# Last slab of down takes its first five weights for both token blocks in turn; x1's transposes at half the rate

## The chip, the cores and the metric

The kernel runs on one core of one Trainium2 chip. Its time is device microseconds of one execution; lower is better. A core has TensorE (PE) for matrix products, with its weight loads listed apart (PEld), VectorE (DVE), ScalarE (ACT), GpSimd (POOL) and SyncE (SP). Here SP issues most of the DMAs, and POOL some. Each engine works through its own instructions strictly in order: an instruction that waits holds up all that stand behind it.

## The reference, cut to what matters

One residual block, float32, 2048 tokens of 1024 channels. The part that the change touches is the second half: the down projection, the norm behind it and the residual.

```python
x = x + rmsnorm(merged @ w_o[l], norm_mix_post[l])        # called x1 below
h = rmsnorm(x, norm_mlp_pre[l])
f = jnp.square(jax.nn.relu(h @ w_up[l])) @ w_down[l]      # 2048x4096 @ 4096x1024
x = x + rmsnorm(f, norm_mlp_post[l])
```

Ahead of it stand one combined input projection of the normed x, a pooling branch, a convolution branch, and their gated sum `merged`.

## The kernel before, in words

**Tiling.** Tokens come in two blocks b of 1024, each of two halves t of 512 (T); rows g of a half are 128 tokens. Matrix products follow a fast 2x2 scheme of seven products i = 1 to 7, whose operands are a block or a sum of blocks of the weight and of the tokens. For precision each operand is a high part plus a low part, both of a type that TensorE takes at full pace, and three of the four partial products are computed (high by high, high by the tokens' low, the weight's low by high).

**down.** Its 4096 rows are four slabs s, the last of which is `LAST`. A slab has 7 products for each token block. The list `jobs` (1898) is the order of all of them; its first entry is done earlier, so that 55 jobs remain, the last 14 of them in the last slab. A job is two halves h of 24 matmuls, 48 in all (`token_product`, the matmul is L1708). It takes two weight tiles o = 0, 1 and two token cells j. A weight tile is a raw tile `wr` that SP loads, ACT's cast of it to `wh` (L209 before the last slab, L1647 in it), and a low part `wl`: in the earlier slabs DVE subtracts it (L123), and in the last slab SP loads it from `lows` in DRAM, where `last_weights` (1570) has put it, with weight sums in `wsum`. A token cell is a load from `fd` into a `tr` buffer, ACT's cast of it (L1688) and DVE's subtraction into the same `tr` buffer (L123). Cells are prepared two jobs ahead in the last slab, one ahead elsewhere. Buffers rotate: 5 `wr`, 3 `wh`, 3 `wl`, 9 `tr`, 28 `big`, 5 `fo`. All `load` calls go to SP (L129), all `aside` calls to POOL (L133).

**The last slab.** In the earlier slabs each product's sum is added to an accumulator in `acc` by DVE (L120). In the last slab `last_product` (1745) keeps sums open in PSUM, a chain for each h: products 1, 6, 7, 4 go on in one chain, 5 and 3 in another, 2 has its own, and after each product DVE adds the chain as it stands into one quadrant of the output. A quadrant (m, t) is a half m of the channels and a half t of the tokens. `ENDS` names the product after which each quadrant is complete. The jobs of the last slab run all seven products of b = 0, then all seven of b = 1, so each weight is fetched twice. The main loop (1940) asks for both weight tiles of a job right ahead of it.

**Background.** Generators in `lanes` run beside the jobs: after each half job `bg()` steps every lane, so two steps to a job. A step lets a lane advance its generator `rate` times; `yield n` makes it sit out n steps. Two matter here. `turned` (1770) brings x1 from its transposed layout `x1d` into rows `x1t` in 16 rounds: two loads on POOL into a `tr` buffer, a wait of `yield 2`, one transpose on DVE (L1784) into a second `tr` buffer, four stores on POOL. `Finish` (1798) ends one quarter [b, t] of the output: `gain` sums the squares and applies the channel gains for each complete quadrant, `fetch` loads rows of `x1t` into `big` buffers on SP, `root` forms the norm, `cell` (L1831) scales and adds the residual on DVE, `put` stores. `steps` does that for three of the quarters; for [1, 1], `last_steps` prepares and `at_end` finishes inside the last product. Which of the instructions that are ready goes first is settled when the program is built, by priority: weights and cells are put forward (`AHEAD`), background work behind; the engines then run what that gives, in order.

The lines that the change touches:

```python
    DOWN_LAST = (1, 6, 7, 4, 2, 5, 3)                                  # 1566
                        yield 2                                        # 1783
            for g in range(2):                                         # 1846
                self.fetch(g)
    jobs += [(LAST, i, b) for b in range(NB) for i in DOWN_LAST]       # 1901
```

Of the kernel before, what the change touches and what calls it, by code (L numbers as in the profile page):

```python
# [67 lines left out]
def block_kernel(  # L68
# [1496 lines left out]
    DOWN = (5, 6, 1, 3, 7, 4, 2)  # L1565
    DOWN_LAST = (1, 6, 7, 4, 2, 5, 3)
    ENDS = {(0, 0): 2, (1, 0): 4, (1, 1): 5, (0, 1): 3}
    wsum, lows = {}, {}
# [176 lines left out]
    def last_product(i, h, b, w, cells):  # L1745

        if i in (1, 2, 5):
            if i == 5 and b:
                chains[i, h] = [root_psum() if h else psum("down")[:, :T] for _ in (0, 1)]
            else:  # L1750
                tiles[i, h] = psum("down")
                chains[i, h] = banks(tiles[i, h])
        of = {1: 1, 6: 1, 7: 1, 4: 1, 2: 2, 5: 5, 3: 5}[i]
        ps, whole = chains[of, h], tiles.get((of, h))
        final = (i, b) == (DOWN_LAST[-1], 1)
# [14 lines left out]
    def turned():  # L1770
        for b in range(NB):
            for t in (0, 1):
                to = x1t[b, t].rearrange("(n tb i) (q k j) -> n q i tb k j", n=2, i=32, q=4, j=32)
                for c in (0, 2):
                    for n in (0, 1):
                        x, y = mk(*TR), mk(*TR)
                        s = slice(n * (T // 2), (n + 1) * (T // 2))
                        for k in (0, 1):
# [3 lines left out]
                            )  # L1782
                        yield 2
                        nc.vector.transpose(  # L1784
# [13 lines left out]
    class Finish:  # L1798
# [38 lines left out]
        def put(self, g):  # L1837
            (load if self.b else aside)(out[self.b, self.t, g], self.x[g])

        def steps(self, lag):  # L1840
            for k in ((0, 0), (0, 1), (1, 0), (1, 1)) if self.t == 0 else ((1, 0), (1, 1), (0, 0), (0, 1)):
                while k not in self.ready:
                    yield 1
                self.gain(*k)
                yield
            for g in range(2):
                self.fetch(g)
            r = self.root(0, G)
            yield lag
            for g in range(G):  # L1850
                if g + 2 < G:
                    self.fetch(g + 2)
                self.cell(g, r[:, g : g + 1], self.parts(g))
                self.put(g)
                yield

        def last_steps(self):
            for g in range(G):
                self.fetch(g)
            for k in ((1, 0), (1, 1)):  # L1860
                while k not in self.ready:
                    yield 1
                self.gain(*k)
                yield

        def at_end(self, h, c, ps):
# [17 lines left out]
            def after(gg):  # L1884
                with tc.high_priority(offset=URGENT):
                    arrive(gg)
                    if gg:
                        r = self.root(2 * h, 2 * h + 2)
                        for g in (0, 1):
                            leave(2 * h + g, r[:, g : g + 1])  # L1890

# [48 lines left out]
    for n, (s, i, b) in enumerate(jobs):  # L1940
        if s < LAST and i == DOWN[0] and b == 0:
            part = weights_down(s)
        if s == LAST and i == DOWN_LAST[0]:
            part = weights_down(s)
            if b == 0:
# [96 lines left out]
```

## Time and profile before

| what | value |
|---|---|
| time, median of 3 runs | 2176.47 us (2173.34 to 2177.3) |
| the profiled execution's own time | 2174.86 us |
| its span, first to last instruction | 2173.1 us |
| its mean granted TensorE clock | 0.995 |
| PE busy | 2135.3 us, 98%, 9424 matmuls |
| DVE busy | 1716.1 us, 79% |
| ACT busy | 1034.3 us, 48% |
| POOL busy | 74.8 us, 3% |
| DMA | 578.54 MB, mean 266 GB/s |

The span is that of one execution on record, and the trace's times count from its start. Busy shares are averages over stages that differ. The stage of the down products is the last quarter of the span; its rows are read by windows and waits below. In a row of waits the arrow points from what stood still to what released it, `<-`; in an instruction's row, the brackets hold its idle time and what ended it. Queue names with a small q at the end (SPq) mean the issuing of DMAs.

### The profile page before, as it was taken

To read this page: it belongs to the slowest core of one execution; us is meant where nothing else is said; L and a number is where in the kernel's file an instruction comes from. 1 tells how busy PE (TensorE), PEld (TensorE's weight loads), DVE (VectorE), ACT (ScalarE), POOL (GpSimd) and SP (SyncE) were. 2 spreads that over 40 slices of the span, in tenths; PEclk is the share of its full clock that TensorE was granted. 3 is DMA by queue.
4 is the path that set the end of the run, shared out by engine and by line. 5 is a ranking of instruction groups with operands and counts; after the bars stand their busy time and mean duration, and the time that the engine had idled before them with its cause. 6 is when DMAs were issued, how large, how long until landed. Compare 5 with 4: busy or idle time off the path is not lost.

```text
span 2173.1 us, 25018 instructions
## 1 busy us (share of the span) xinstructions
PE 2135.3 (98%) x9424; PEld 1759.1 (81%) x9424; DVE 1716.1 (79%) x1664; ACT 1034.3 (48%) x1119; POOL 74.8 (3%) x131
## 2 busy tenths in 40 slices
PE   9999999999999999999999999999999999999996
PEld 7778888888888888888888888888887788888875
DVE  8999788999789999997777857876655775687557
ACT  6444453334534655445635766665443332223442
POOL 0000000000000000000000000000122300000000
PEclk9999999999999999999999999999999999999998
DMA  4789998688897787336686768986987775445896
GB/s 177 267 301 330 342 353 311 228 286 305 320 342 271 262 303 268 136 116 233 249 335 227 267 249 307 360 284 240 345 277 280 257 257 173 163 145 187 298 365 235
DMA packets 167498, 578.54 MB, mean 266 GB/s; under 512 B 20304, under 2 KB 24528, under 8 KB 167376
## 3 DMA queue, kind: packets, MB, share of 16 engines
q1 hardware_dynamic: 145616, 501.42, 64.4%
q10 hardware_dynamic: 12672, 46.14, 5.5%
q0 software_dynamic: 9088, 29.37, 3.9%
q8 instruction: 74, 1.21, 0.2%
q14 instruction: 48, 0.39, 0.1%
HBM read 381.20 MB, written 195.65 MB: 265 GB/s over the span
## 4 chain that ended last, share of the span: by engine, by line
PE 73%; DVE 9%; DMA 9%; issue 5%; ACT 2%; POOL 1%; SPq 0%; DVEq 0%; ACTq 0%; POOLq 0%
PE up L252 28%; PE down L1708 18%; PE wo L252 7%; PE glu L252 5%; PE B L252 4%; PE ga L252 3%; PE gb L252 3%; DVE y L910 3%; PE pool L252 2%; DMA tr<-x1d 2%; PE A L252 2%; DMA wl<-lows 1%; DMA tr<-fd 1%; POOL x1t L133 1%; DVE wl L123 1%
## 5 line engine op out<-in xcount | busy, mean ns | idle before, releaser
L252 PE MATMUL up<-big,wh 128*128 128x512 f32 x1792 | 480.9, 390 | 1.2 <-DVE big L123 0.8
L252 PEld LDWEIGHTS up<-big,wh 128*128 128x128 f32 x1792 | 335.8, 188 | 71.9 <-DVE big L123 1.1
L209 ACT CAST wh<-wr 128x1024 fp32r<-128x1024 f32 x167 | 175.5, 1052 | 314.9 <-PE up L252 68.5
L1708 PE MATMUL down<-wh,tr 128*128 128x512 f32 x784 | 307.0, 392 | 3.2 <-DVE tr L123 3.2
L910 DVE SCALAR_TENSOR_TENSOR y<-v,cst,y 128x1024 f32<-128x1024 f32 x240 | 307.0, 1279 | 2.4
L1708 PE MATMUL down<-wh,fo 128*128 128x512 f32 x776 | 298.6, 390 | 0.5 <-ACT wh L209 0.5
L252 PE MATMUL up<-big,wl 128*128 128x512 f32 x896 | 275.9, 389 | 0.0
L1708 PE MATMUL down<-wl,fo 128*128 128x512 f32 x760 | 235.1, 391 | 3.0 <-DVE wl L123 3.0
L209 ACT CAST wh<-ws 128x1024 fp32r<-128x1024 f32 x124 | 130.5, 1053 | 220.1 <-PE up L252 74.7
L252 PEld LDWEIGHTS up<-big,wl 128*128 128x128 f32 x896 | 168.2, 188 | 35.1
L1688 ACT CAST fo<-tr 128x1024 fp32r<-128x1024 f32 x86 | 90.4, 1051 | 219.2 <-DMA tr<-fd 90.8
L123 DVE TENSOR_TENSOR wl<-ws,wh 128x1024 fp32r<-128x1024 f32 x116 | 141.4, 1219 | 46.8 <-ACT wh L209 46.3
L1708 PEld LDWEIGHTS down<-wh,tr 128*128 128x128 f32 x784 | 148.0, 189 | 35.2 <-DVE tr L123 4.3
L1708 PEld LDWEIGHTS down<-wh,fo 128*128 128x128 f32 x776 | 145.9, 188 | 31.4 <-ACT wh L209 0.9
L1708 PEld LDWEIGHTS down<-wl,fo 128*128 128x128 f32 x760 | 142.7, 188 | 34.6 <-DVE wl L123 5.3
L123 DVE TENSOR_TENSOR wl<-wr,wh 128x1024 fp32r<-128x1024 f32 x111 | 135.1, 1218 | 26.0 <-ACT wh L209 22.9
L120 DVE TENSOR_TENSOR big<-big,down 128x1024 f32<-128x1024 f32 (+1 forms) x84 | 99.8, 1189 | 70.4 <-PE down L1708 70.3
L123 DVE TENSOR_TENSOR tr<-tr,fo 128x1024 fp32r<-128x1024 f32 x86 | 104.7, 1219 | 46.2 <-ACT fo L1688 46.0
L252 PE MATMUL glu<-big,wh 128*128 128x512 f32 x432 | 117.5, 393 | 3.0 <-ACT tr L408 2.5
L252 PE MATMUL wo<-big,wh 128*128 128x512 f32 x448 | 120.2, 390 | 0.0
L252 PE MATMUL gb<-big,wh 128*128 128x512 f32 x448 | 120.1, 390 | 0.0
L252 PE MATMUL ga<-big,wh 128*128 128x512 f32 x448 | 119.8, 389 | 0.0
(208 smaller groups left out, 3383.0 us busy)
## 6 DMA issues: line engine op xcount, KB each, us to landing
tr<-fd SPq DMA_DIRECT2D x110, 512.0 KB, 4.5
wr<-w_down SPq DMA_DIRECT2D x68, 512.0 KB, 6.3
wl<-kept SPq DMA_DIRECT2D x67, 512.0 KB, 5.2
kept<-wl SPq DMA_DIRECT2D x66, 512.0 KB, 5.7
wr<-w_up SPq DMA_DIRECT2D x64, 512.0 KB, 4.5
wr<-w_in SPq DMA_DIRECT2D x56, 512.0 KB, 6.0
fd<-tr ACTq DMA_DIRECT2D x54, 512.0 KB, 3.5
fd<-tr SPq DMA_DIRECT2D x48, 512.0 KB, 3.3
```

What stands on the lines that cost most here:

```text
L120: return nc.vector.tensor_tensor(o, a, b, op=ALU.add)
L123: return nc.vector.tensor_tensor(o, a, b, op=ALU.subtract)
L133: return nc.gpsimd.dma_start(o, src)
L209: nc.scalar.copy(hi[:, :n], src[:, :n])
L252: i = nc.tensor.matmul(ps, w[wp][:, (at + k) * P : (at + k + 1) * P], rhs[k][xp], start=start and n == 0, stop=stop and n == len(order) - ...
L910: nc.vector.scalar_tensor_tensor(acc, v[:, k : k + TB], wk, acc, op0=ALU.mult, op1=ALU.add)
L1688: nc.scalar.copy(hi, t)
L1708: i = nc.tensor.matmul(ps[gg], cells[j][xp][:, c * T + at : c * T + at + P], w[j][wp][:, c * T : (c + 1) * T], start=start and first, stop ...
```

## The change

The last slab's products are ordered 2, 1, 6, 7, 4, 5, 3. The first five are run for b = 0 and b = 1 in turn with one fetch of the weight; then 5, 3 for b = 0 and 5, 3 for b = 1, with a fetch each. For that, PSUM chains are kept for each (i, h, b): while 1, 6, 7, 4 run, four are open, and the chain of b = 1, h = 1 lies in two separate banks, whose sums are added in two halves. `ENDS` takes for each quadrant the product that comes later in the new order.

In `turned`, the wait of a round becomes `yield 4`. `steps` loads three rows ahead in place of two and drops the wait `lag` of the quarters [0, 0] and [0, 1]. Stores of b = 0 go to POOL and those of b = 1 to SP, as before, by another call. `last_steps` loads its four rows two at a time, after each gain, with steps between. The branch in `at_end` that was rewritten issues the same calls in the same order. The lanes of all four quarters start with the first job of the last slab, [0, 0], [1, 0], [0, 1] in one lane of rate 3 and [1, 1] in one of rate 2; before, the two of b = 1 started with b = 1.

```diff
-    DOWN_LAST = (1, 6, 7, 4, 2, 5, 3)
-    ENDS = {(0, 0): 2, (1, 0): 4, (1, 1): 5, (0, 1): 3}
+    DOWN_LAST = (2, 1, 6, 7, 4, 5, 3)
+    ENDS = {(0, 0): max((1, 2), key=DOWN_LAST.index), (1, 0): 4, (0, 1): 3, (1, 1): max((5, 7), key=DOWN_LAST.index)}
...
         if i in (1, 2, 5):
-            if i == 5 and b:
-                chains[i, h] = [root_psum() if h else psum("down")[:, :T] for _ in (0, 1)]
+            tiles.pop((i, h, b), None)
+            if (i == 5 and b and h == 0) or (b and h):
+                chains[i, h, b] = [root_psum() if h else psum("down")[:, :T] for _ in (0, 1)]
             else:
-                tiles[i, h] = psum("down")
-                chains[i, h] = banks(tiles[i, h])
+                tiles[i, h, b] = psum("down")
+                chains[i, h, b] = banks(tiles[i, h, b])
...
-        if i == 5 and b:
+        if whole is None:
             for q, half in zip(ps, banks(c)):
                 mark(add(half, half, q))
...
-                        yield 2
+                        yield 4
                         nc.vector.transpose(
...
         def put(self, g):
-            (load if self.b else aside)(out[self.b, self.t, g], self.x[g])
+            (nc.gpsimd if self.b == 0 else nc.sync).dma_start(
+                out[self.b, self.t, g], self.x[g]
+            )
...
-            for g in range(2):
+            for g in range(3):
                 self.fetch(g)
             r = self.root(0, G)
-            yield lag
+            if lag:
+                yield lag
             for g in range(G):
-                if g + 2 < G:
-                    self.fetch(g + 2)
+                if g + 3 < G:
+                    self.fetch(g + 3)
...
         def last_steps(self):
-            for g in range(G):
-                self.fetch(g)
-            for k in ((1, 0), (1, 1)):
+            for n, k in enumerate(((1, 0), (1, 1))):
                 while k not in self.ready:
                     yield 1
                 self.gain(*k)
+                yield
+                self.fetch(2 * n)
+                yield
+                self.fetch(2 * n + 1)
                 yield
...
-    jobs += [(LAST, i, b) for b in range(NB) for i in DOWN_LAST]
+    jobs += [(LAST, i, b) for i in DOWN_LAST[:5] for b in range(NB)]
+    jobs += [(LAST, i, b) for b in range(NB) for i in DOWN_LAST[5:]]
...
-                lanes += [Lane(3, fin[0, 0].steps(3), fin[0, 1].steps(3))]
-            else:
-                lanes += [Lane(2, fin[1, 0].steps(1)), Lane(2, fin[1, 1].last_steps())]
-        if s == LAST or b == 0 or (s, i) in [(0, i) for i in FIRST]:
+            if (i, b) == (DOWN_LAST[0], 0):
+                lanes += [Lane(3, fin[0, 0].steps(0), fin[1, 0].steps(1), fin[0, 1].steps(0)), Lane(2, fin[1, 1].last_steps())]
+        if (s == LAST and not (b and i in DOWN_LAST[:5])) or b == 0 or (s, i) in [(0, i) for i in FIRST]:
             w = [part(i, o) for o in (0, 1)]
```

How the instructions move shows in the order in which each engine gets them. In these rows a name is that of a buffer pool with numbers of its tile. First DVE, in the first third of the down products, before: three of the transposes (L1784) stand within eleven rows.

```order
L1784 STREAM_TRANSPOSE tr_2792_12887<-tr_2791_12886 128x4x8x32
L123 TENSOR_TENSOR wl_2810_12999<-wr_2808_12996,wh_2809_12998 128x1024
L123 TENSOR_TENSOR tr_2811_13002<-tr_2811_13002,fo_2812_13004 128x1024
L123 TENSOR_TENSOR tr_2813_13007<-tr_2813_13007,fo_2814_13009 128x1024
L123 TENSOR_TENSOR wl_2837_13161<-ws_2833_13154,wh_2836_13160 128x1024
L123 TENSOR_TENSOR ws_2833_13154<-ws_2833_13154,wr_2865_13326 128x1024
L1784 STREAM_TRANSPOSE tr_2802_12960<-tr_2801_12959 128x4x8x32
L123 TENSOR_TENSOR tr_2822_13077<-tr_2821_13075,tr_2822_13077 128x1024
L123 TENSOR_TENSOR tr_2821_13075<-tr_2822_13077,fo_2823_13080 128x1024
L123 TENSOR_TENSOR tr_2825_13085<-tr_2824_13083,tr_2825_13085 128x1024
L1784 STREAM_TRANSPOSE tr_2818_13045<-tr_2817_13044 128x4x8x32
```

Behind the change, about the same place of the program has one transpose in eleven rows (its line is now 1785):

```order
L1785 STREAM_TRANSPOSE tr_2784_12851<-tr_2783_12850 128x4x8x32
L123 TENSOR_TENSOR tr_2789_12886<-tr_2789_12886,fo_2790_12888 128x1024
L123 TENSOR_TENSOR tr_2801_12957<-tr_2801_12957,fo_2802_12959 128x1024
L123 TENSOR_TENSOR wl_2800_12954<-wr_2798_12951,wh_2799_12953 128x1024
L123 TENSOR_TENSOR tr_2803_12962<-tr_2803_12962,fo_2804_12964 128x1024
L123 TENSOR_TENSOR wl_2825_13107<-ws_2821_13100,wh_2824_13106 128x1024
L123 TENSOR_TENSOR ws_2821_13100<-ws_2821_13100,wr_2851_13263 128x1024
L123 TENSOR_TENSOR tr_2812_13032<-tr_2811_13030,tr_2812_13032 128x1024
L123 TENSOR_TENSOR tr_2811_13030<-tr_2812_13032,fo_2813_13035 128x1024
L123 TENSOR_TENSOR tr_2815_13040<-tr_2814_13038,tr_2815_13040 128x1024
L123 TENSOR_TENSOR wl_2830_13117<-ws_2826_13110,wh_2829_13116 128x1024
```

What stands between two transposes are the low parts of weights (`wl`) and of tokens (`tr`) of two products, where it was those of one. The number of transposes, 16, is unchanged.

Second SP, in the middle of the last slab, before. `wl<-lows` are low parts of weights, a pair of them for each job; `tr<-fd` are token cells, `wr<-wsum` raw weights:

```order
L129 DMA wl_3150_15351<-lows_2493_11403 128x1024
L129 DMA wl_3157_15417<-lows_2357_10857 128x1024
L129 DMA tr_3171_15498<-fd_1774_8201 128x1024
L129 DMA wr_3177_15572<-wsum_2229_10349 128x1024
L129 DMA wr_3180_15578<-wsum_2392_10995 128x1024
L129 DMA tr_3173_15503<-fd_1829_8486 128x1024
L129 DMA wl_3160_15423<-lows_2516_11492 128x1024
L129 DMA wl_3167_15489<-lows_2382_10952 128x1024
```

Between the second row and the last two lies one job's worth of loads. The changed program at the corresponding place:

```order
L129 DMA wl_3147_15343<-lows_2454_11232 128x1024
L129 DMA tr_3167_15490<-fd_1783_8245 128x1024
L129 DMA wl_3163_15481<-lows_2259_10478 128x1024
L129 DMA wr_3189_15744<-w_down 128x1024
L129 DMA wr_3192_15750<-w_down 128x1024
L129 DMA tr_3169_15495<-fd_1836_8524 128x1024
L129 DMA tr_3171_15550<-fd_2564_11748 128x1024
L129 DMA tr_3173_15555<-fd_2625_12037 128x1024
L129 DMA wl_3166_15487<-lows_2427_11135 128x1024
```

Two jobs' token cells now stand between one low part and the next pair; the second low part of a pair follows the first with a cell between.

Third SP near the end, before. `big<-x1t` are row loads of `fetch`:

```order
L129 DMA tr_3281_16125<-fd_2612_11983 128x1024
L129 DMA wl_3275_16111<-lows_2382_10952 128x1024
L129 DMA big_3227_15818<-x1t_200_188 128x1024
L129 DMA wr_3285_16191<-wsum_2229_10349 128x1024
L129 DMA wr_3288_16197<-wsum_2392_10995 128x1024
L129 DMA big_3229_15852<-x1t_196_186 128x1024
L129 DMA big_3230_15854<-x1t_196_186 128x1024
L129 DMA wr_3309_16302<-wsum_2302_10632 128x1024
L129 DMA wr_3312_16308<-wsum_2463_11272 128x1024
L129 DMA big_3261_15995<-x1t_196_186 128x1024
L129 DMA big_3262_16000<-x1t_196_186 128x1024
L129 DMA wl_3278_16117<-lows_2533_11568 128x1024
```

and after it, where L1839 is the store of `put`:

```order
L129 DMA big_3228_15983<-x1t_198_187 128x1024
L129 DMA big_3229_15985<-x1t_198_187 128x1024
L129 DMA wl_3248_16055<-lows_2474_11319 128x1024
L129 DMA big_3230_15987<-x1t_198_187 128x1024
L129 DMA wl_3269_16167<-lows_2242_10399 128x1024
L129 DMA big_3242_16035<-x1t_198_187 128x1024
L1839 DMA out<-big_3228_15983 128x1024
L1839 DMA out<-big_3229_15985 128x1024
L1839 DMA out<-big_3230_15987 128x1024
L129 DMA wl_3272_16173<-lows_2403_11039 128x1024
L129 DMA wl_3281_16254<-lows_2313_10676 128x1024
L1839 DMA out<-big_3242_16035 128x1024
```

Before, five row loads and four raw weights stand in one run ahead of the last low part shown, the second of the twelfth job. Now row loads stand among low parts, and three stores of the quarter [1, 0] stand ahead of `wl_3272`, the second low part of the thirteenth job.

More of the change, by code (lines that the diff above doesn't have):

```diff
@@ L1747, in last_product @@
         if i in (1, 2, 5):
-            if i == 5 and b:
-                chains[i, h] = [root_psum() if h else psum("down")[:, :T] for _ in (0, 1)]
-            else:
-                tiles[i, h] = psum("down")
-                chains[i, h] = banks(tiles[i, h])
+            tiles.pop((i, h, b), None)
+            if (i == 5 and b and h == 0) or (b and h):
+                chains[i, h, b] = [root_psum() if h else psum("down")[:, :T] for _ in (0, 1)]
+            else:
+                tiles[i, h, b] = psum("down")
+                chains[i, h, b] = banks(tiles[i, h, b])
         of = {1: 1, 6: 1, 7: 1, 4: 1, 2: 2, 5: 5, 3: 5}[i]
-        ps, whole = chains[of, h], tiles.get((of, h))
+        ps, whole = chains[of, h, b], tiles.get((of, h, b))
         final = (i, b) == (DOWN_LAST[-1], 1)
@@ L1886, in after @@
                     arrive(gg)
-                    if gg:
-                        r = self.root(2 * h, 2 * h + 2)
+                    if h:
+                        if gg:
+                            r = self.root(2, 4)
+                            for g in (2, 3):
+                                leave(g, r[:, g - 2 : g - 1])
+                    elif gg:
+                        r = self.root(0, 2)
                         for g in (0, 1):
-                            leave(2 * h + g, r[:, g : g + 1])
+                            leave(g, r[:, g : g + 1])
             return after
@@ L1942, in block_kernel @@
             part = weights_down(s)
-        if s == LAST and i == DOWN_LAST[0]:
+        if s == LAST and i == DOWN_LAST[0] and not b:
             part = weights_down(s)
-            if b == 0:
+        if s == LAST:
+            if (i, b) == (DOWN_LAST[0], 0):
                 gains.append(mk(p_ws, "ws"))
```

1 line of the change is left out of this document (added).

## The prediction, made before the changed kernel was run

> **What bounds the kernel now.** I read the waits of the matmul queue first, over everything from the first of the down products to the end; the columns are total us, number, longest.
>
> ```profile
> PE down L1708 <- DMA wl<-lows: 8.0, 3, 6.2
> PE down L1708 <- DVE tr L123: 3.2, 2, 1.8
> PE down L1708 <- DVE wl L123: 3.0, 4, 1.3
> PE down L1708 <- ACT wh L209: 0.5, 1, 0.5
> ```
>
> TensorE is the bound: in 620 us it waits 14.7 us. The windows by stage say where, and that the waits cost more than themselves. Columns: length, then busy time and count of PE, PEld, DVE, ACT and POOL, then granted clock, DMA share and GB/s.
>
> ```profile
> 1800.00:1890.00 90.00, 90.00 (x399) 74.53 (x398) 55.41 (x49) 26.31 (x26) 0.00 (x0) 1.00 0.49 162
> 1600.00:1800.00 200.00, 193.28 (x837) 157.29 (x836) 121.64 (x104) 68.52 (x70) 46.95 (x75) 0.99 0.76 258
> 1800.00:2000.00 200.00, 200.00 (x885) 165.58 (x884) 148.38 (x129) 59.88 (x59) 0.00 (x0) 1.00 0.48 159
> 2050.00:2140.00 90.00, 81.98 (x347) 66.33 (x346) 53.82 (x70) 37.97 (x59) 4.34 (x8) 0.96 0.89 334
> ```
>
> An undisturbed stretch holds 885 matmuls in 200 us, 0.226 us each, so a product of 48 takes 10.85 us. **Stretch A**, 1600 to 1800, is 48 short: 10.8 us lost, of which 3.2 + 3.0 + 0.5 = 6.7 are waits and 4.1 a lower clock after them. **Stretch B**, 2050 to 2140 in the last slab, is 52 short: 11.7 us lost, 8.0 of it waits. Both lie on the path that sets the end, since TensorE does nothing else meanwhile. That is 22.5 us, the ceiling of what this change can win outside the tail.
>
> Stretch A is traced back through the in-order queues. One stall as an example, PE, DVE and POOL:
>
> ```profile
> 1653.68 0.50 PE L1708 MATMUL down<-wh,tr 128*128 128x512 f32 x1 [1.80 <-DVE tr L123]
> 1651.27 1.25 DVE L1784 STREAM_TRANSPOSE tr<-tr 128x1024 f32<-128x1024 f32 x1 [3.32 <-DMA tr<-x1d]
> 1638.32 1.76 POOL L133 DMA_DIRECT2D x1t<-tr  x3 [3.54 <-DVE tr L1784]
> 1643.42 0.58 POOL L133 DMA_DIRECT2D x1t<-tr  x1 [3.34 <-issue]
> 1647.22 0.73 POOL L133 DMA_DIRECT2D tr<-x1d  x1 [1.16 <-DVE tr L123]
> DVE tr L1784 <- DMA tr<-x1d: 29.6, 8, 6.2
> L1784 DVE STREAM_TRANSPOSE tr<-tr x16: 1233/1245/1247, 1549.2 to 1747.7; 128x1024 f32<-128x1024 f32 x16
> ```
>
> POOL issues a round's four stores, stands 3.34 us before the fourth, then issues the next round's second load at 1647.22; it lands when the transpose starts, at 1651.27. DVE has stood at that transpose for 3.32 us, and the low part that TensorE needs is behind it in DVE's order. Eight transposes stand so, 29.6 us together. The sixteen start from 1549.2 to 1747.7: a round takes 198.5 / 15 = 13.2 us, while its lane wants one every product, 10.85 us. The rounds are late by their own chain, and DVE pays.
>
> Stretch B is in the chain of work that ended last:
>
> ```profile
> 2058.67 6.99 DMA wl<-lows
> 2065.70 15.73 PE down L1708 x68
> 2081.45 7.40 DMA wl<-lows
> 2088.89 26.85 PE down L1708 x116
> 2115.76 12.44 DMA wl<-lows
> 2128.25 14.31 PE down L1708 x50
> 2065.70 0.73 PE L1708 MATMUL down<-wl,big 128*128 128x512 f32 x2 [0.72 <-DMA wl<-lows]
> 2128.25 1.22 PE L1708 MATMUL down<-wl,big 128*128 128x512 f32 x2 [6.17 <-DMA wl<-lows]
> ```
>
> The low part of a product's second weight can be loaded only once the same buffer is released, three quarters into the product before. From issue to use are 6.99 - 0.72 = 6.3 us, and 12.44 - 6.17 = 6.3 us again. A landing above 6.3 us is a stall. These rows of SP show why the third landed so late, and the issues of the last 194 us what is usual (last column, median us to landing):
>
> ```profile
> 2107.71 0.43 SPq L129 DMA_DIRECT2D big<-x1t  x1
> 2108.24 0.87 SPq L129 DMA_DIRECT2D wr<-wsum  x2
> 2109.16 1.40 SPq L129 DMA_DIRECT2D big<-x1t  x2
> 2110.66 1.19 SPq L129 DMA_DIRECT2D wr<-wsum  x2
> 2113.07 1.54 SPq L129 DMA_DIRECT2D big<-x1t  x2
> wl<-lows SPq DMA_DIRECT2D x27, 512.0 KB, 4.6
> big<-x1t SPq DMA_DIRECT2D x16, 512.0 KB, 9.3
> ```
>
> Nine transfers of 512 KB, none urgent, went out in the 8 us ahead of an urgent one.
>
> **The change, part by part.** *Transposes at half the rate.* Same sixteen transposes, loads and stores; one round in two products, 21.7 us, instead of one in 10.85. The chain of a round takes 13.2 us, so a load has landed some 8 us before its transpose, and the 29.6 us of DVE's waits go. What is late next: the tr buffers, nine in rotation. A pair is held twice as long, but half as many pairs are taken, and from the order of the changed kernel a load that needs a pair's buffer still has about two products until its use, as before. Two stalls of stretch A had no waiting transpose ahead of them:
>
> ```profile
> 1714.95 0.73 PE L1708 MATMUL down<-wl,fo 128*128 128x512 f32 x2 [0.85 <-DVE wl L123]
> 1760.03 0.72 PE L1708 MATMUL down<-wl,fo 128*128 128x512 f32 x2 [1.26 <-DVE wl L123]
> ```
>
> They come from cells loaded late, which the transposes' buffers delay but not alone; I leave their 2.1 us standing. So A gives 10.8 - 2.1 = **8.7 us** (ends: 0, if the waits only move; 10.8). The seven or so rounds that now fall after 1760 add 1.245 us each to DVE, which has 200 - 148.38 = 51.6 us free in 1800 to 2000; without that cover they would cost 9 us.
>
> What a leftover stall costs is open, for these rows show the clock (third-last column) after one:
>
> ```profile
> 1686.00:1690.00 4.00, 2.12 (x9) 1.00 0.84 246
> 1690.00:1692.00 2.00, 2.00 (x6) 0.55 0.76 252
> 1689.56 0.50 PE L1708 MATMUL down<-wh,tr 128*128 128x512 f32 x1 [1.40 <-DVE tr L123]
> ```
>
> Here the clock fell to 0.55 after a wait of 1.40 us, so short waits can cost twice. The Trainium skill, "TensorE: Matmul & The Clock Gate", section "What's actually happening", says that the clock halves after an idle window of about 3.4 us; by it, waits as short as these would not lower it. By that rule removing A's waits returns 6.7 us and not the 4.1 beside them, and the sum would be 2159.1; the trace disagrees, since its fall came without such a window.
>
> *Weights kept for two products.* Five weights are fetched once and not twice: 5 x 2 tiles x (raw and low) = 20 transfers, 10.5 MB less. Ten second-weight loads with 6.3 us of grace become five, and in front of each of them the changed order has single cell loads, not row loads. At the 4.6 us median there is 1.7 us to spare, so the stalls at 2065 and 2088 (0.8 and 1.4 us or so) go. The 12.44 us landing goes because its nine transfers are no longer in a row: row loads stand in fours or fewer, behind weights and with two thirds of a product between them and the next urgent one. Four of 512 KB at the 334 GB/s of stretch B take 6.3 us, and three quarters of a product is 8.1. I leave 0.5 us: **11.2 us** (ends: 0, if another landing takes the place; 11.7).
>
> *Four chains open.* The matmul count is the same, 14 x 48. A bank is written again two products after its sum, not one, so DVE's add has more grace. The fourth chain lies in two separate banks and is added in halves, which rows of the last slab price:
>
> ```profile
> 2144.32 0.68 DVE L120 TENSOR_TENSOR big<-big,down 128x512 f32<-128x512 f32 x1
> 2138.50 1.22 DVE L120 TENSOR_TENSOR big<-big,down 128x1024 f32<-128x1024 f32 x1 [2.44 <-PE down L1708]
> ```
>
> Five times 2 x 0.68 - 1.22 = 0.14 us, 0.7 in all, beside a DVE that is busy 53.82 of 90 us; uncovered, 0.7 us.
>
> *The finish.* Quarter [1,0] of the output now ends four products before the end and [0,1] two before it (before: two and seven). Its row loads, root, cells and stores go with it. The final instructions are the same calls; the last matmul ends at 2159.61 + 0.61 and the span at 2173.1:
>
> ```profile
> 2159.61 0.61 PE L1708 MATMUL rb<-wl,big 128*128 128x512 f32 x2
> span 2173.1 us, 25018 instructions
> ```
>
> I take the tail of 12.9 us as unchanged (ends: 1.4 less, two cells of DVE that stood among the last sums; 1.3 more, a cell that waits there for its rows).
>
> **The sum**, against the profiled execution's own 2174.86 us, which lies 1.6 below the median of the runs: 2174.86 - 8.7 - 11.2 = 2155.0. I do not carry the 1.6; the three runs shown differ by 4.0.
>
> **Rivals.** *R1, a late low part after all.* On SP the second low weight of the thirteenth product now stands behind three stores of [1,0], each of which waits for DVE's cells, and those for row loads. Speaking for it: DVE's longest wait for row loads.
>
> ```profile
> DVE big L1831 <- DMA big<-x1t: 11.7, 3, 7.8
> ```
>
> Against it: these rows are asked for a product earlier, 10.85 us, and landed in 9.3. If it happens once at the size of the worst landing, 6.2 us and 3 of slow clock, the time is 2164. The Trainium skill, "DMA: Bandwidth & Descriptors", section "Anatomy of one DMA", fits about 2.0 us plus bytes / 436e3 to a transfer issued from GpSimd; an estimate by that page for a low part behind three stores is 2.0 + 4 x 1.2 = 6.8 us, a wait of 0.5 and 2155.5, and for nine ahead 14 against the 12.44 here.
>
> *R2, the transposes keep their waits.* It decides if a round grows from 13.2 to over 21.7 us, or if buffers held longer delay the cells as much as now. For it: DVE is busier after 1800 (148 of 200 us against 122). A then gives nothing: 2163.7.
>
> *R3, the low clock stays* though the waits go: A's 4.1 remain, 2159.1. Speaking for it are only the 0.99 against 1.00 of the windows.
>
> *R4, slower.* The cells of [1,0] and [0,1], eight row loads, stand in DVE's order ahead of adds that free banks for the last four products. If each row load makes DVE wait 7.8 us, that is 62 us; DVE's idle share in B, 40% of the 43 us of four products, hides 17, and 45 come out: 2155 + 45 = 2200. It beats the gain of 19.9 by more than 4.4 us from a mean wait of (24.3 + 17) / 8 = 5.2 us. Against it: 3.9 was the mean here of three, with DMA at 0.89, and the change takes 10.5 MB from that stretch.
>
> **How the numbers follow.** Forecast 0.66 at 2155.0, its own range 2152 to 2160. R1 0.14, R2 0.09, R3 0.04. R1 and R2 together, with a second late landing, 0.03, about 2172 and no change that can be told. R4 0.04. The range, 2152 to 2165, takes the ceiling at its low end and R1, R2 and R3 at its high end; about 2 in 10 stay out. Differences under 0.2%, 4.4 us, cannot be told from none by a measurement of this kernel. Faster 0.92, same 0.04, slower 0.04.
>
> **What would show it.** In the changed profile DVE's waits at the transposes for x1d should be near nothing, the matmul queue's waits for DVE in stretch A under 2.5 us, and its waits for the low weights under 1 us; the matmuls of 200 us from 1600 should be 875 or more. The last low loads should land in under 6.3 us. R1 shows as a wait at the second weight of one of the last four products, with stores ahead on SP; R2 as the same x1d waits later; R4 as waits of TensorE for L120 adds. I would be wrong if the stalls of A come mainly from cells that are late for another reason.

## The result, and the profile after

| | before | changed |
|---|---|---|
| time, median (range) of 4 runs each | 2176.76 us (2173.34 to 2177.3) | 2154.47 us (2152.06 to 2155.57) |
| ratio, 95% interval | | 0.9899 (0.9882 to 0.9916) |
| profiled execution: its time, its span | 2174.86, 2173.1 us | 2155.38, 2153.6 us |

The change is 1.0% faster; the forecast was 2155.0 us, in a range of 2152 to 2165. TensorE's waits in the changed kernel, over the same part of the program (total us, number, longest), are all of these:

```profile
PE down L1708 <- DMA wl<-lows: 0.3, 1, 0.3
PE down L1708 <- DVE st L120: 0.3, 1, 0.3
```

They were 14.7 us. The windows of the changed kernel, with the columns of the prediction:

```profile
1600.00:1800.00 200.00, 200.00 (x884) 165.61 (x883) 121.94 (x105) 70.23 (x70) 33.82 (x54) 1.00 0.70 244
2050.00:2140.00 90.00, 89.39 (x394) 73.35 (x393) 66.05 (x102) 38.49 (x73) 4.35 (x8) 1.00 0.82 301
```

Both stretches now run at the undisturbed pace, 884 matmuls where it was 837, and 394 where it was 347. VectorE's waits at the transposes went from 29.6 us to a single one:

```profile
DVE tr L1785 <- DMA tr<-x1d: 3.0, 1, 3.0
```

The issues of the last 174 us (number, size, median us to landing):

```profile
wl<-lows SPq DMA_DIRECT2D x17, 512.0 KB, 5.5
big<-x1t SPq DMA_DIRECT2D x16, 512.0 KB, 7.1
```

Low weights are 17 in this stretch where they were 27 in the 194 us before. One of the signs that I had set did not come true throughout: the low part behind the wait of 0.3 us took longer than 6.3 us to land (start, us, in the chain of work):

```profile
2104.47 7.17 DMA wl<-lows
```

**Three marks that compare kernels.** The end of the up products, where down takes over, differs by some 8 us between the profiled executions below (1537.2 to 1545.7), in code that no edit names, so their times say less than lengths between marks. I take the end of the last up matmul, the start of DVE's 58th addition of a down sum to an accumulator, and the end of the last matmul. In the timeline of the kernel before:

```profile
1538.98 0.39 PE L252 MATMUL up<-big,wl 128*128 128x512 f32 x1
2006.99 1.22 DVE L120 TENSOR_TENSOR big<-big,down 128x1024 f32<-128x1024 f32 x1 [1.65 <-PE down L1708]
2159.61 0.61 PE L1708 MATMUL rb<-wl,big 128*128 128x512 f32 x2
```

and of the changed one:

```profile
1540.95 0.39 PE L252 MATMUL up<-big,wl 128*128 128x512 f32 x1
1998.39 1.22 DVE L120 TENSOR_TENSOR big<-big,down 128x1024 f32<-128x1024 f32 x1 [2.16 <-PE down L1708]
2140.39 0.61 PE L1708 MATMUL rb<-wl,big 128*128 128x512 f32 x2
```

"Front" is from the first mark to the second (nearly all of the first three slabs and a little of the last), "last slab" from the second to the third, "tail" from there to the span's end. The front went from 467.62 to 457.05 us, the last slab from 153.23 to 142.61, the tail from 12.88 to 12.60: 10.57 + 10.62 + 0.28 = 21.5 us won, of which the spans show 19.5, since this execution began down 1.97 later.

### The profile page after: what moved, and what is told of

It reads as the page before. It is cut to its first block, busy times and chain, and to the rows that moved or that the text cites. A ratio compares the mean times of both kernels' runs of the same rounds, so it can differ in the third digit from the quotient of the medians.

```text
span 2153.6 us, 24989 instructions
## 1 busy us (share of the span) xinstructions
PE 2130.3 (99%) x9424; PEld 1758.8 (82%) x9424; DVE 1717.0 (80%) x1669; ACT 1024.5 (48%) x1109; POOL 74.8 (3%) x131
## 4 chain that ended last, share of the span: by engine, by line
PE 85%; DVE 8%; DMA 3%; issue 2%; ACT 1%; SPq 0%; DVEq 0%; ACTq 0%
PE up L252 28%; PE down L1708 26%; PE wo L252 7%; PE glu L252 4%; PE B L252 4%; PE gb L252 4%; PE A L252 4%; PE ga L252 3%; DVE y L910 3%; PE pool L252 3%; PE rb L1708 1%; DVE tr L120 1%; DVE wl L123 1%; DMA kept<-ws 1%; PE rb L458 1%
## 5 line engine op out<-in xcount | busy, mean ns | idle before, releaser
L1708 PE MATMUL down<-wh,fo 128*128 128x512 f32 x756 | 290.3, 389 | 0.3 <-DVE st L120 0.3
L1708 PE MATMUL down<-wh,tr 128*128 128x512 f32 x744 | 289.4, 389 | 0.0
L1708 PE MATMUL down<-wl,fo 128*128 128x512 f32 x740 | 227.8, 389 | 0.0
L123 DVE TENSOR_TENSOR wl<-ws,wh 128x1024 fp32r<-128x1024 f32 x116 | 141.6, 1220 | 48.5 <-ACT wh L209 46.9
L1708 PEld LDWEIGHTS down<-wh,tr 128*128 128x128 f32 x744 | 139.6, 188 | 28.9
L123 DVE TENSOR_TENSOR wl<-wr,wh 128x1024 fp32r<-128x1024 f32 x111 | 135.2, 1219 | 25.6 <-ACT wh L209 22.6
L123 DVE TENSOR_TENSOR tr<-tr,fo 128x1024 fp32r<-128x1024 f32 x86 | 103.8, 1221 | 56.4 <-ACT fo L1688 55.9
L120 DVE TENSOR_TENSOR big<-big,down 128x1024 f32<-128x1024 f32 (+1 forms) x79 | 94.0, 1190 | 60.4 <-PE down L1708 60.0
```

What stands on the lines that cost most here:

```text
L120: return nc.vector.tensor_tensor(o, a, b, op=ALU.add)
L123: return nc.vector.tensor_tensor(o, a, b, op=ALU.subtract)
L1708: i = nc.tensor.matmul(ps[gg], cells[j][xp][:, c * T + at : c * T + at + P], w[j][wp][:, c * T : (c + 1) * T], start=start and first, stop ...
```

## The experiments

Median and range are those of a run's executions; the ratio is to the kernel before in the same session. The lengths are those of one execution each, in us.

| run | time, us | ratio (95%) | front | last slab | tail |
|---|---|---|---|---|---|
| rate_only | 2165.06 (2161.47 to 2171.51) | 0.9953 (0.9936 to 0.9970) | 457.10 | 150.26 | 12.79 |
| old_rate | 2165.53 (2162.62 to 2170.09) | 0.9955 (0.9938 to 0.9972) | 466.97 | 143.06 | 12.92 |
| rate_rows | 2159.62 (2155.65 to 2163.89) | 0.9923 (0.9906 to 0.9940) | 457.09 | 146.87 | 13.16 |
| twice | 2160.96 (2158.78 to 2168.05) | 0.9936 (0.9918 to 0.9954) | 457.10 | 152.01 | 12.83 |
| ahead | 2173.36 (2169.67 to 2177.75) | 0.9992 (0.9978 to 1.0005) | 468.68 | 149.54 | 12.92 |
| rate3 | 2169.22 (2164.89 to 2174.40) | 0.9977 (0.9962 to 0.9992) | 470.55 | 142.21 | 12.60 |
| old_rows | 2161.77 (2158.50 to 2163.64) | 0.9939 (0.9921 to 0.9958) | 457.07 | 143.88 | 18.04 |
| twice_early | 2155.77 (2155.09 to 2157.09) | 0.9914 (0.9898 to 0.9930) | 457.07 | 145.28 | 12.58 |
| late | 2183.39 (2180.43 to 2187.10) | 1.0041 (1.0024 to 1.0057) | 457.69 | 170.81 | 12.51 |
| ahead4 | 2160.21 (2158.04 to 2162.26) | 0.9938 (0.9916 to 0.9960) | 460.01 | 142.89 | 13.17 |
| early | 2152.80 (2152.51 to 2155.97) | 0.9909 (0.9883 to 0.9935) | 457.07 | 142.38 | 12.53 |
| one_buf | 2170.46 (2168.13 to 2174.70) | 0.9980 (0.9969 to 0.9991) | 462.57 | 152.00 | 12.54 |

### Do the two halves stand alone? (rate_only, old_rate)

rate_only is the kernel before with one line changed, old_rate the changed kernel with that line put back:

```diff
-                        yield 2
+                        yield 4
```

> The kernel before, with the transposes at half the rate and nothing else of the change. Theory: the stalls of stretch A (1600 to 1800) came from rounds that want to start every 10.85 us and need 13.2; they go, and the last slab keeps its 11 us. 2174.9 - 8.7 = 2166 us (2164 to 2168), DVE's waits at the transposes for x1d under 3 us (29.6 before), TensorE's longest wait for a low weight in the last slab still 5 to 7 us. Rival (the rounds only take their waits with them past 1800): 2171 or more, x1d waits over 15 us.

> The changed kernel with the transposes back at the old rate (a wait of 2 steps). Theory: the two halves of the change don't touch each other, so stretch A loses its 8.7 us again and the last slab keeps its gain: 2155.4 + 8.7 = 2164 us (2162 to 2166), x1d waits near 30 us, low weights under 1 us. Rival (part of the last slab's gain hangs on the later transposes, or the other way round): more than 2 us away from that.

They do. The front follows the rate alone: 457.10 with half of it, 466.97 with the old one, whatever the last slab does. The last slab keeps its gain with the old rate (143.06) and loses it without the new order (150.26; a bit less than the 153.23 of before, in unchanged code). Both times lie in the range expected; the one wait left at a transpose is 3.5 us, a little over the 3 that I had set. Waits of rate_only, TensorE's and VectorE's:

```profile
PE down L1708 <- DMA wl<-lows: 6.3, 2, 5.6
DVE tr L1784 <- DMA tr<-x1d: 3.5, 1, 3.5
```

### Why do the rounds disturb? (ahead, rate3, late, ahead4, one_buf)

In **ahead**, from the kernel before, a round's loads go out a round earlier, at the old rate:

```diff
+            x = nxt
+            if r + 1 < len(rounds):
+                nxt = get(*rounds[r + 1])
             yield 2
+            y = mk(*TR)
             nc.vector.transpose(
```

> The kernel before, transposes at the old rate, but the two loads of a round go out one round earlier, ahead of the stores of the round between. Measured by the stretch from the end of the last up product to DVE's 58th add into the accumulators: 467.6 us before, 457.05 in the changed kernel. Theory (a round's own chain of 13.2 us is too long for a rate of one in 10.85, since its loads stand behind the stores of the round before): the stretch is 457 to 459, x1d waits under 5 us, the time some 10 us under the kernel before, about 2165. Rival (what hurts is the rate itself: the transfers or the nine tr buffers): 463 to 468.

The theory of the prediction missed. VectorE waits for no x1d load any more, yet the front is no shorter, 468.68. The waits of ahead up to 1990, of VectorE and of TensorE:

```profile
DVE tr L123 <- DMA tr<-fd: 12.5, 5, 5.2
DVE tr L1792 <- DMA x1t<-tr: 7.1, 2, 6.7
PE down L1708 <- DVE tr L123: 4.1, 3, 2.2
PE down L1708 <- ACT fo L1688: 2.2, 2, 1.1
```

Now token cells (`tr<-fd`) land late, and a transpose waits for a `tr` buffer that is still being stored from. What a late cell costs hangs on the place: the same row of VectorE's waits (`tr` L123 for `tr<-fd`) reads 10.0 us in the kernel before, up to 1990, and 10.0 in the changed one, where TensorE felt none of them.

**rate3** is the changed kernel with `yield 3`:

> The changed kernel with a round every 3 steps, 16.3 us in place of 21.7. Theory: any period above the chain's 13.2 us will do: the same stretch is 457 to 458 us, x1d waits under 5 us, the time that of the changed kernel, 2153 to 2157. Rival (the chain gets longer under load, or cells are late because of the buffers): 460 or more and 2158 or more.

A miss again, and the worst front of all, 470.55, with two thirds of the old rate. TensorE's waits in it are 7.3 us, not much above the 6.7 of before; but the granted clock was 0.66 from 1655 to 1665 and 0.72 from 1696 to 1702, which is 5.1 us lost, where before lost 1.7. Its first large stall in the rows of SP, DVE and PE:

```profile
1633.52 12.04 SPq L129 DMA_DIRECT2D wr<-w_down  x4
1645.67 4.36 SPq L129 DMA_DIRECT2D tr<-fd  x6
1653.40 1.23 DVE L123 TENSOR_TENSOR tr<-tr,tr 128x1024 f32<-128x1024 f32 x1 [8.19 <-DMA tr<-fd]
1655.75 0.50 PE L1708 MATMUL down<-wh,fo 128*128 128x512 f32 x1 [2.90 <-ACT fo L1688]
```

SP stands 12 us among four raw weights, behind which the build put the six loads of token cells (why it put them there is open). No transpose is among these causes, and no `tr` buffer either: SP's longest wait there was of 8.6 us, for VectorE's low part of a weight. So late cells are what TensorE feels, and the `tr` buffers, nine, of which a round takes two, became the suspect by ahead and not by this stall.

**late** starts the lane at the third slab, at the old rate. There a token cell needs one `tr` buffer; in the front's first part it often needs two.

```diff
-        if n == 1:
+        if n == 27:
             lanes.append(Lane(2, turned()))
```

> The kernel before, transposes at the old rate of one a product, but started at the third slab of down, where a token cell needs one tr buffer and not two. Stretch as before, from the end of the last up product to DVE's 58th add: 467.6 us before, 457.05 in the changed kernel, 468.7 with the loads a round ahead, 470.6 with a round every 3 steps. Theory now (TensorE's stalls come from token cells that get their tr buffer late, and a round holds two of the nine): 457 to 460, though DVE still stands 10 to 35 us at the transposes, since the chain of a round is unchanged. Rival (the chain of a round that is longer than its turn, as the prediction had it): 465 to 470 again. The last slab is no concern here; a few rounds may reach into it.

The front is 457.69, nearly clean. Its transposes between 1850 and 1945 as a group (shortest, median and longest in ns, first and last start):

```profile
L1784 DVE STREAM_TRANSPOSE tr<-tr x9: 1235/1237/1239, 1853.1 to 1941.6; 128x1024 f32<-128x1024 f32 x9
```

and the window of that part (length, busy time and count of PE, PEld, DVE, ACT and POOL, clock, DMA share, GB/s):

```profile
1850.00:1990.00 140.00, 140.00 (x619) 115.93 (x618) 122.66 (x107) 39.13 (x38) 45.86 (x73) 1.00 0.72 231
```

From the first to the last of nine transposes are 88.5 us, 11.06 us from one to the next, and not one waits (three later ones do, after 1990). The same chain of loads, transpose and stores that took 13.2 us keeps up with nearly 10.85 here, under a like DMA share (0.72, where stretch A had 0.76). Its length was no fixed property of it, then. Waiting for buffers is the likely cause that stretched it, but not shown to be: a cell of the third slab also takes one load in place of two, and POOL stood 57.0 us ahead of its stores in the 16 rounds of before (22 times) for nothing that the profile names, against 28.5 us (17 times) in late between 1830 and 2000, for 14 rounds. The time is worse than before because TensorE stood 10.7 and 6.0 us early in the last slab, where the rounds that were left are drained together, with a granted clock of 0.50 behind them (2016 to 2020).

**ahead4** is ahead in the changed kernel: half the rate, but a loaded buffer held one round longer.

> The changed kernel, one round in two products, with its two loads a round earlier, so that a loaded tr buffer is held some 20 us longer and no transpose can wait for its load. Theory (tr buffers): cells get late again, the stretch is 460 to 466 us with DVE's waits at the transposes for x1d under 2 us. Rival (the chain of a round): 457 to 457.5.

No transpose waits for a load, and still the front loses 2.96 us: the low end of what the buffers made one expect, and more than the chain would allow. But of TensorE's three waits there (0.5, 0.5 and 0.7 us) only one is behind a cell in a `tr` buffer, so this is weak support.

**one_buf** is the kernel before with each round on one buffer:

```diff
-                        x, y = mk(*TR), mk(*TR)
+                        x = y = mk(*TR)
...
-                            y.rearrange("p (tb k j) -> p k tb j", k=4, j=32),
+                            x.rearrange("p (k tb j) -> p k tb j", k=4, j=32),
                             x.rearrange("p (k tb j) -> p k tb j", k=4, j=32),
```

> The kernel before at the old rate, with each transpose written back into the tr buffer that it reads, so that a round holds one of the nine buffers and not two. (The blocks of x1 then lie in the wrong places of the rows, so the residual that is added is another; the work is the same.) DVE's order, the loads and the stores stay. Same stretch: 467.6 us before, 457.05 at best. Theory (buffers): 457 to 461, the time 2164 to 2168. Rival (the chain of a round, its loads behind the stores of the round before): 465 to 468, DVE's waits at the transposes for x1d still 25 us or more, the time 2172 to 2175. Both: in between.

In between, and the sharpest of the five. VectorE's waits at the transposes are no less than they were (29.1 us for loads, and 7.4 more without a named cause), and the front loses 5.5 us in place of 10.6:

```profile
DVE tr L1784 <- DMA tr<-x1d: 29.1, 6, 6.0
PE down L1708 <- DVE tr L123: 2.3, 2, 1.2
PE down L1708 <- DVE wl L123: 1.5, 2, 1.3
```

One buffer of nine given back is half of the loss; the other half is open to both causes, since a round on one buffer still shares the pool.

The link from rounds to cells stands in SP's own waits. SP issues the token cells, in order with all its other loads. These are its waits, from 1540 to 1990, until a round's stores out of a `tr` buffer had landed, in before and in the changed kernel:

```profile
SPq L129 <- DMA x1t<-tr: 71.0, 15, 10.5
SPq L129 <- DMA x1t<-tr: 6.9, 1, 6.9
```

In old_rate they are 71.5 us, in ahead 38.6, in one_buf 38.3, in rate3 29.8, in ahead4 10.8. So a round's buffers do hold back the loads of cells, and half the rate ends that. How much of the front's loss comes that way the sums don't say: rate3 has the worst front with less than half of before's.

### Where does the last slab's gain come from? (rate_rows, twice, old_rows, twice_early, early)

**rate_rows**: the kernel before with the half rate and the changed row loads, old order, each weight fetched twice.

```diff
-            for g in range(2):
+            for g in range(3):
                 self.fetch(g)
...
-                if g + 2 < G:
-                    self.fetch(g + 2)
+                if g + 3 < G:
+                    self.fetch(g + 3)
...
-            for g in range(G):
-                self.fetch(g)
-            for k in ((1, 0), (1, 1)):
+            for n, k in enumerate(((1, 0), (1, 1))):
...
+                yield
+                self.fetch(2 * n)
+                yield
+                self.fetch(2 * n + 1)
                 yield
```

> The kernel before, with half the transpose rate and the changed row loads (three ahead, the last quarter's staggered behind its gains), but the old order of products, each weight fetched twice, two chains. Theory: the 12.44 us landing came from nine non-urgent transfers in a row; now five stand there, so that stall of 6.2 us and its 2.9 us of low clock go, while the two of about 1 us stay: 2166 - 9 = 2157 us (2156 to 2160). Rival (the weights fetched twice are the cause): the long wait stays, 2165 to 2167.

As the theory had it: the long stall is gone, the small ones stay, and one behind VectorE is new. The last slab takes 146.87 us; unchanged, it took 149.5 to 153.2 in four executions (before, rate_only, ahead, one_buf), so the row loads are worth 2.7 to 6.4 (3.4 against rate_only, from which it differs in nothing else).

```profile
PE down L1708 <- DMA wl<-lows: 2.6, 3, 1.4
PE down L1708 <- DVE tr L123: 1.6, 1, 1.6
```

**twice**: the changed kernel, but each weight is fetched for each block.

```diff
-        if (s == LAST and not (b and i in DOWN_LAST[:5])) or b == 0 or (s, i) in [(0, i) for i in FIRST]:
+        if s == LAST or b == 0 or (s, i) in [(0, i) for i in FIRST]:
```

> The changed kernel with its order of products and its four chains, but each of the first five weights fetched again for the second block: 20 transfers of 512 KB come back. Theory: sharing the weights is worth only the two stalls of about 1 us, and up to six transfers now stand ahead of an urgent low part: 2156 to 2159 us (changed kernel 2154.5), waits for low weights 1 to 3 us in total. Rival 1 (sharing is what the last slab's gain comes from): 2162 to 2166, waits for low weights 5 us or more. Rival 2 (sharing is worth nothing): 2154 to 2155.

Slower than the theory, and not by the rival's cause: the waits for low weights come to 1.4 us. The chain of work shows what it was (start, us), with the two rows of VectorE and TensorE that stood:

```profile
2092.55 8.65 DMA big<-x1t
...
2102.63 2.27 DVE tr L123 x2
2104.90 2.65 DVE big L1832 x4
2107.55 1.13 DVE big L120
...
2108.83 11.36 PE down L1708 x37
2101.22 1.41 DVE L1832 SCALAR_TENSOR_TENSOR big<-big,sy,big 128x512 f32<-128x512 f32 x2 [4.38 <-DMA big<-x1t]
2108.83 0.77 PE L1708 MATMUL down<-wh,fo 128*128 128x512 f32 x1 [4.59 <-DVE st L120]
```

A row load lands 8.65 us after its issue; VectorE stands 4.38 us at the cell that needs it; the addition that frees a bank is behind that cell, and TensorE waits 4.59 us for the bank, with a granted clock of 0.50 from 2108 to 2114. That is the rival R4 of the prediction, in one place. In the changed kernel the wait of PE at about the same place, and the only other one, read:

```profile
2107.45 0.47 PE L1708 MATMUL down<-wh,fo 128*128 128x512 f32 x1 [0.30 <-DVE st L120]
2111.68 0.73 PE L1708 MATMUL down<-wl,big 128*128 128x512 f32 x2 [0.31 <-DMA wl<-lows]
```

There VectorE is late by 0.30 us with no wait for rows at all. So the place has next to no slack, and sharing the weights seems to pay by letting the row loads land, more than by its own two small stalls; the next run puts that to the test.

**twice_early** asks for the first three rows of a quarter ahead of its gains, in twice; **early** does so in the changed kernel.

```diff
+            for g in range(3):
+                self.fetch(g)
             for k in ((0, 0), (0, 1), (1, 0), (1, 1)) if self.t == 0 else ((1, 0), (1, 1), (0, 0), (0, 1)):
...
-            for g in range(3):
-                self.fetch(g)
```

> The new order with each weight fetched for each block (as in the run before, whose last slab took 152.0 us and in which TensorE stood 4.6 us behind DVE while DVE stood 4.4 us at a row load), now with the first three rows of each quarter asked for ahead of its gains instead of behind them. Theory (R4's mechanism: rows that land late hold DVE, and DVE's adds hold the banks): the wait for DVE falls under 1.5 us and the last slab takes 144 to 147 us. Rival (DVE is late by its own amount of work): it stays over 3 us and 149 to 153.

It holds: the wait for VectorE falls to 1.0 us, the last slab from 152.01 to 145.28. What sharing adds beyond early rows is the rest, 145.28 to the 142.38 of early: three waits for low weights, 1.6 us together, 0.8 us less of the wait for VectorE, and what each wait costs beside itself.

> The changed kernel with the first three rows of each quarter asked for ahead of its gains. What is left in its last slab are two waits of 0.3 us, one of them behind DVE at the bank of the thirteenth product. Theory (rows that land earlier let DVE pass): the last slab takes 142.0 to 142.6 us (142.6 in the changed kernel), the time 2152 to 2156, not to be told from the changed kernel. Rival (big buffers held longer delay something else): 143.5 or more.

142.38 us, and 2152.80, which cannot be told from the changed kernel. It is the lowest median of all.

**old_rows**: the changed kernel with the finish of before.

```diff
-            for g in range(3):
+            for g in range(2):
                 self.fetch(g)
             r = self.root(0, G)
-            if lag:
-                yield lag
+            yield lag
...
-                lanes += [Lane(3, fin[0, 0].steps(0), fin[1, 0].steps(1), fin[0, 1].steps(0)), Lane(2, fin[1, 1].last_steps())]
+                lanes += [Lane(3, fin[0, 0].steps(3), fin[1, 0].steps(1), fin[0, 1].steps(3)), Lane(2, fin[1, 1].last_steps())]
```

(with `g + 2` again, and the old `last_steps`)

> The changed kernel with the row loads of before: two ahead, the pause of the quarters [0, 0] and [0, 1], and all four rows of the last quarter at once, which now falls into the first product of the last slab. Measured by the stretch from DVE's 58th add to the last matmul: before 153.2 us, changed kernel 142.6, old order with the new row loads 146.9, new order without sharing 152.0. Theory (sharing the weights gives SP and DVE the room; the row edits are worth little beside it): 142.5 to 144.5, time 2153 to 2157. Rival (DVE now stands at rows asked for only two ahead, and TensorE behind it for a bank): DVE's waits for x1t over 8 us, 146 or more, 2158 or more.

The last slab is where the theory put it, 143.88, and the rival's wait for rows is 1.2 us; yet the time is 7 us above the changed kernel, which neither had. The tail is 18.04. The last matmul ended at 2143.56, and VectorE then still had all eight half cells of [0, 1] to do, with the last quarter's behind them:

```profile
2144.27 0.74 DVE L1832 SCALAR_TENSOR_TENSOR big<-big,sy,big 128x512 f32<-128x512 f32 x1
2145.60 0.74 DVE L1832 SCALAR_TENSOR_TENSOR big<-big,sy,big 128x512 f32<-128x512 f32 x1
2146.34 4.06 DVE L1832 SCALAR_TENSOR_TENSOR big<-big,sy,big 128x512 f32<-128x512 f32 x6
```

The quarter [0, 1] ends two products before the end in the new order; paced as before, its cells fall behind the last sums. The old finish costs 5.4 us of tail against the changed kernel and 5.2 against before, so that of the 9.35 us won in the last slab over before 4.2 are left. The run doesn't part the pause from the rows asked for two ahead.

## Why the prediction was right, point by point

**Transposes at half the rate**, put at 8.7 us, gave 10.57 (10.5 in rate_only). That the waits go was right. Two steps behind it were not. The cause named, a round's own chain of 13.2 us against a turn of 10.85, fell in ahead and rate3 and with the 11.06 us of late; the 13.2 was the mean time from one transpose to the next, so a pace, and never the length of a chain. What the runs leave is that rounds and token cells share nine `tr` buffers, and that cells come late: SP stood 71.0 us for the rounds' stores. That this is all of the loss is argued and not shown. R2's second condition ("buffers held longer delay the cells as much as now") was thus the right place to look, though the half rate is far enough from it. And the 2.1 us that I left standing, for two stalls with no waiting transpose ahead, went too: both came behind late cells (one held VectorE 4.01 us at 1705, one ScalarE 8.54 us at 1751), which the half rate ended with the rest.

**What a stall costs** beside its wait was put wholly to the clock: 4.1 us in stretch A. Part of it stands at each wait. The second and third of these rows of before show it:

```profile
1686.56 0.61 PE L1708 MATMUL down<-wl,fo 128*128 128x512 f32 x2
1687.66 0.50 PE L1708 MATMUL down<-wh,fo 128*128 128x512 f32 x1 [0.48 <-ACT wh L209]
1689.90 0.40 PE L1708 MATMUL down<-wh,fo 128*128 128x512 f32 x1
```

From 1686.56, two matmuls at 0.227 us and the wait of 0.48 lead to 1687.49, and the next starts at 1687.66; 1689.90 follows a start at 1689.56 by 0.34. A wait so costs about 0.28 us more than the trace gives for it, part of that because it counts a single matmul as longer (0.39 us) than the 0.227 at which they follow each other. By this one stall as the estimate for all, 7 x 0.28 = 2.0 us in stretch A; the slow clock, 4 us at 0.57 from 1690, adds some 1.7. The sum, 6.7 + 2.0 + 1.7 = 10.4, is close to the 10.57 that the front won.

**Weights kept for two products**, put at 11.2 us, gave 10.62. The term holds two causes that I had apart only in words. Row loads out of the way are worth 2.7 to 6.4, and the rest (146.87 to 142.61) comes with order and sharing together: the order alone, without sharing, made it worse (152.01 in twice). The nine transfers in a row were read rightly: with five (rate_rows), the longest wait fell from the 5.6 of rate_only to 1.4 us. Left over are waits of 0.3 + 0.3 us and what the two cost beside themselves; I had left 0.5.

**The tail**, taken as unchanged, became 0.28 us shorter, but only because the finish was changed along with the order: the upper end that I gave it, 1.3 us more, does not hold the 5.2 more of old_rows.

**Rivals.** R1 did not come: SP issued the three stores from 2111.65 and the two low weights behind them from 2116.56, and TensorE waited for neither. R3 did not come: the clock went with the waits. R4's mechanism is real and was closer than I had it: I asked for a mean wait of 5.2 us over eight loads before it beat the gain; twice shows one wait of 4.38 us for a row holding TensorE for 4.59, and then the slow clock.

That 2155.0 lies 0.5 us from the median is luck in part, better than the terms deserve: A was 1.9 short, the last slab 0.6 over, the tail 0.3 short, and the profiled execution began down 2.0 later than that of before.

## What to carry to other kernels

Background work that draws on the same rotating buffers as the loads of the critical path can be paid for in late loads, not in the waits that it shows itself; read the waits of the queue that issues those loads, and try whether one buffer less per round moves the stall, before blaming the round. Between an urgent load and the one before it count the transfers, and let big unhurried loads go out a product early. When an order is changed so that work ends later, look at what paces the work behind it: it was set for the old end.

## What the runs showed of the hardware

The granted clock can fall after short waits that stand close together. In before, 0.48 and then 1.40 us of waiting within 2.4 us were followed by 4 us at 0.57, while a single wait of 1.80 us at 1653 left it at 1.00. But in ahead 1.09 and then 0.76 us within 2.4 us, up to 1612.2, left it at 1.00 too, so their sum alone does not settle it (window, length, PE's busy time and count, clock, DMA share, GB/s; the last row is of ahead):

```profile
1690.00:1694.00 4.00, 4.00 (x12) 0.57 0.63 220
1653.00:1657.00 4.00, 3.32 (x15) 1.00 0.82 251
2132.00:2134.00 2.00, 2.00 (x7) 0.52 0.01 4
1612.00:1616.00 4.00, 3.79 (x16) 1.00 0.88 346
```

The third row is the end of the slow part behind the wait of 6.17 us, which lasted about 6 us from there. The Trainium skill, "TensorE: Matmul & The Clock Gate", section "What's actually happening", ties the fall to an idle window of about 3.4 us; in the first of these rows it came behind 1.88 us in two pieces, and 1.85 us in two pieces did not bring it in the last. What parts the two no run here shows.
